# Feed-forward weight sums moved from POOL to DVE, and more eight-product blocks, in a two-layer diffusion step

## The chip, the core and the metric

The kernel runs on one core of one Trainium2 chip. The time is the device time of one execution in microseconds (us), and less is better. The core has a matrix engine (PE, with its weight loads shown as PEld), three engines for element-wise work (DVE, ACT and POOL), and queues that issue transfers; SP issues nearly all of them here. Each engine works through its own instructions in a fixed order, and waits at an instruction until the results that it needs are there.

## The reference, cut to what matters

One inference step of a two-layer backbone over 640 tokens: 512 latent tokens and 128 prompt tokens, which have a modulation of their own. Every layer is a mixer followed by a SwiGLU feed-forward part:

```python
def ada_modulation(cond, w_mod, b_mod):
    m = jax.nn.silu(cond) @ w_mod + b_mod          # 1024 -> 6 * 1024, one vector per group and layer
    return jnp.split(m, 6, axis=-1)                # sh1, sc1, g1, sh2, sc2, g2

def swiglu(h, w_in, w_out):
    gate, up = jnp.split(h @ w_in, 2, axis=-1)     # w_in 1024 x 5632, w_out 2816 x 1024
    return (jax.nn.silu(gate) * up) @ w_out

for l in range(2):
    ...
    hp = modulate(rms_norm(xp, norm_mix[l]), sh1_p, sc1_p)
    ...                                            # mixer: MLA + neighbourhood attention, or GQA
    hp = modulate(rms_norm(xp, norm_ffn[l]), sh2_p, sc2_p)
    xp = xp + g2_p * swiglu(hp, w_ffn_in[l], w_ffn_out[l])   # the same for the latent tokens xs
```

Everything is float32. The outputs are both streams after a final norm, and the context tensors of the two mixers.

## The kernel before, in words

**Arithmetic.** Tokens lie on the free axis (640 columns, two halves of 320), features on the 128 partitions, 1024 features in 8 tiles. A float32 product is made of three matmuls in a reduced 32-bit format: every operand is split into a high part (ACT copies it into that format) and a low part (DVE or POOL subtracts the high part from the source), and `mm3` adds high*high, high*low and low*high.

**Feed-forward, first half (`ffn`).** The 2816 hidden features are 22 blocks of 128. A block needs gate and up, each for two halves of the tokens and 8 tiles of features.

- The first `FEW` = 2 blocks of each layer take the plain way, eight products of four tiles: 2 (gate, up) x 2 (halves) x 8 (tiles) x 3 = 96 matmuls of 320 columns. Only the two raw weight tiles of 128 x 1024 are split (`unit`, L161 to L170).
- The other 20 blocks take seven products of four tiles (a Winograd scheme over gate and up, halves of the features and halves of the tokens): 7 x 4 x 3 = 84 matmuls. For that the weights are also added up: `s13` and `s24`, four additions of 128 x 512 on POOL (L1117, L1118, L1121, L1122), and `wX`, `wY`, `wZ`, `wW` are split (L1034, L1035, L1114, L1115). The activations are added up once a layer (`ModS.add_up`, L296 to L303, into the tiles D, C, N and E), between matmuls of block 0 in the order of the source.
- A block ends with a silu on ACT, the product `sg` (L1084 or L1098 on DVE), its split into `hd` (L1055 on ACT, L1056 on DVE), and, for most blocks, two transfers to DRAM (L1061, "spill"), since the chip's memory does not hold all of the hidden features.

`ModS.make` produces the activations of each half (`i` = 0, 1) that the products read: DVE multiplies by the norm (L280), ACT applies scale and shift (L283), and the split is on DVE (L289, L290) for even tiles and on POOL (L286, L287) for odd ones. The second half (`i` = 1) is made while PE is in block 0.

**Modulation as side work.** The modulation vectors of layer 1, and the last gate of layer 0, are not made by PE but by DVE, beside the feed-forward part: 48 weight tiles in layer 0 and 8 in layer 1. Each is loaded (`wm`, 512 KB), multiplied by the broadcast condition `cb`, and summed over its row by two instructions (`junk`, L1265). `mod_side` holds the list, and `step("fb", fb)` at the end of a block, or `step("n", i)` in the output layer, takes as many tiles as the plan says. `cb` lies where `ModS` keeps half of its sums, so that it can be loaded only after `add_up`.

**Rooms.** Raw weight tiles, `wm` among them, go through a ring of three rooms (tag `raw` of `rawp`); the second raw tile of a seven-product block has two rooms of its own (`wr`). Split weights have three rooms in `wp` and three in a pool that lives as long as the first half (`fp`); a plain block past the first takes both of its tiles from `wp`.

**Feed-forward, second half.** `wout` loads and splits the output weights in two passes over the 8 tiles of features (9 and 13 hidden blocks), alternating between `wp` and a pool `fo` that can open only when `fp` is free.

**Order.** The source gives dependencies and priorities. A planner then simulates the program with estimated durations, and writes out a fixed order for every engine and for every queue; where the thing first in the source is expected late, it puts other work ahead. Transfers of SP are issued in that fixed order too, each after the room that it fills is free.

Of the kernel before, what the change touches and what calls it, by code (L numbers as in the profile page):

```python
# [18 lines left out]
P = 128  # L19
# [29 lines left out]
def body(ctx, tc, xT, vecs, crow, wm0, wm0g, wm1, wA, wNV, wNA, wMK, wMV, wOA, wGQ, wGK, wGV, wOC,  # L49
# [3 lines left out]
    V, S, G = nc.vector, nc.scalar, nc.gpsimd  # L53
# [110 lines left out]
    def unit(src, n, name, lo="v", pool=None):  # L164

        raw = load(src, n, name + "r")
        t = (pool or wp).tile([P, 2, 1024], F32R, tag="w", bufs=3, name=name)
        hi, lw = t[:, 0, :n], t[:, 1, :n]
        S.activation(hi, raw, AF.Copy)
        (V if lo == "v" else G).tensor_tensor(lw, raw, f(hi), ALU.subtract)  # L170
        return hi, lw
# [77 lines left out]
    class ModS:  # L249
# [26 lines left out]
        def make(self, i, rs, k):  # L276
            h, l = self.hl(k, i)
            c0, c1 = HALF[i]
            t = tp.tile([P, HT], F32, tag="u", bufs=7, name=f"{self.name}t{k}{i}")
            V.tensor_tensor(t, self.x[k][:, c0:c1], rs[:, c0:c1], ALU.mult)  # L280
            h32 = (self.left, self.right)[i][k]
            for a0, a1, c in HCOND[i]:
                self.act[k, i] = S.activation(h32[:, a0 - c0:a1 - c0], t[:, a0 - c0:a1 - c0], AF.Identity,  # L283
                                              bias=self.ml[:, self.sh + k, c:c + 1], scale=self.gsl[:, k, c:c + 1])
            if k % 2:
                G.tensor_scalar(h, h32, 1.0, 0.0, ALU.mult, ALU.add)  # L286
                G.tensor_tensor(l, h32, f(h), ALU.subtract)  # L287
            else:
                V.tensor_copy(h, h32)  # L289
                V.tensor_tensor(l, h32, f(h), ALU.subtract)  # L290

        def add_up(self, k):
            left = [self.left[j] for j in (k, k + 4)]
            b12, b22 = self.right[k], self.right[k + 4]
            n = tp.tile([P, HT], F32, tag="u", bufs=7, name=f"{self.name}n{k}")
            V.tensor_tensor(b22, b22, b12, ALU.subtract)  # L296
            V.scalar_tensor_tensor(n, b22, -1.0, left[0], ALU.mult, ALU.subtract)
            V.tensor_tensor(left[0], left[0], b12, ALU.subtract)
            V.scalar_tensor_tensor(left[1], n, -1.0, left[1], ALU.mult, ALU.subtract)
            for c, src in zip("DNCE", (left[0], n, b22, left[1])):  # L300
                t = self.sums[c][k]
                S.activation(t[:, 0:HT], src, AF.Copy)
                (V if c in "DN" else G).tensor_tensor(t[:, HT:T], src, f(t[:, 0:HT]), ALU.subtract)  # L303

    def residual(xo, xi, ps, ml, g, n, i):

# [261 lines left out]
    for kk in range(4):  # L568
        wh, wl = unit(wNV[kk], 1024, f"wnv{kk}")
        for j in range(2):  # L570
            k = 2 * kk + j
# [432 lines left out]
                box["m"].make(c, nrm.rs, k)  # L1004
        return box, nxt

    FEW = 2
    STAY = 3
    FIRST, SECOND = FO_ORDER[:9], FO_ORDER[9:]

# [15 lines left out]
    def ffn(l, x, pend, hm, nxt, side, opened):  # L1026
        ph, fk, dr, hd, fs, fp, w0, _ = opened
        turn = [0]
# [9 lines left out]
        def whole(ps, wt, k, c, first, last):  # L1038
            a, b = [w[:, k * P:k * P + P] for w in wt]
            mm3(ps[:, :HT], a, b, *hm.hl(k, c), first, last)  # L1040
# [23 lines left out]
                kept[fb] = dh, dl  # L1064

        step = None
        for fb in range(FEW):
            pg, pu = [bank(f"fg{l}_{fb}{c}") for c in range(2)], pair(f"fu{l}_{fb}")
            g_, u_ = w1 if fb else w0
            for c in range(2):  # L1070
                for k in range(KT):
                    if fb == 0 and c == 0 and k == 3:
                        pend()
                        step = side(fk, hm.act[7, 1])
                        w1 = [after(hm.act[3 + 2 * i, 1], lambda: unit(wFI[l, 1, i], 1024, f"wgu{l}_1{i}")) for i in range(2)]
                        for j in range(4):
                            hm.add_up(j)
                    for ps, wt in ((pg, g_), (pu, u_)):
                        whole(ps[c], wt, k, c, k == 0, k == KT - 1)
            sg = tmp(f"sg{l}_{fb}")  # L1080
            for c, (c0, c1) in enumerate(HALF):
                after(hm.act[7, 1], lambda: S.activation(sg[:, c0:c1], pg[c][:, :HT], AF.Silu))
            for c, (c0, c1) in enumerate(HALF):
                V.tensor_tensor(sg[:, c0:c1], pu[c][:, :HT], sg[:, c0:c1], ALU.mult)  # L1084
            hidden(fb, sg)
            step("fb", fb)
# [13 lines left out]
            step("fb", fb)  # L1100

        job = None
        for fb in range(FEW, FB):

            ru = load(wFI[l, fb, 1], 1024, f"wu{l}_{fb}r")
            if fb == FEW:
                rg = load(wFI[l, fb, 0], 1024, f"wg{l}_{fb}r")
            else:
                rg = fp.tile([P, 1024], F32, tag="wr", bufs=2, name=f"wg{l}_{fb}r")
                nc.sync.dma_start(rg, wFI[l, fb, 0])  # L1110
            wX = split(ru, f"wX{l}_{fb}")
            t = fp.tile([P, 2, 512], F32R, tag="w4", bufs=2, name=f"wW{l}_{fb}")
            wW = t[:, 0, :], t[:, 1, :]
            S.activation(wW[0], rg[:, 512:], AF.Copy)  # L1114
            V.tensor_tensor(wW[1], rg[:, 512:], f(wW[0]), ALU.subtract)  # L1115
            s13 = fp.tile([P, 1024], F32, tag="ws", bufs=2, name=f"s13{l}_{fb}")
            G.tensor_tensor(s13[:, :512], rg[:, :512], rg[:, 512:], ALU.add)  # L1117
            G.tensor_tensor(s13[:, 512:], ru[:, :512], rg[:, :512], ALU.add)  # L1118
            wY = split(s13, f"wY{l}_{fb}")
            s24 = fp.tile([P, 1024], F32, tag="ws", bufs=2, name=f"s24{l}_{fb}")  # L1120
            G.tensor_tensor(s24[:, :512], s13[:, 512:], rg[:, 512:], ALU.add)  # L1121
            G.tensor_tensor(s24[:, 512:], s24[:, :512], ru[:, 512:], ALU.add)  # L1122
            wZ = split(s24, f"wZ{l}_{fb}")

            g, b5, b2 = bank(f"fg{l}_{fb}"), bank(f"fd{l}_{fb}"), bank(f"fu{l}_{fb}", "y")
            up, sg = tmp(f"up{l}_{fb}"), tmp(f"sg{l}_{fb}")
            p1, p5, u1, g2 = [utile(f"{n}{l}_{fb}") for n in ("p1", "p5", "u1", "g2")]
            product(g, wX, 0, 11, True)
            S.activation(p1, g[:, :HT], AF.Copy)  # L1129
            product(b5, wY, 0, "D", True)  # L1130
            S.activation(p5, b5[:, :HT], AF.Copy)
            if job:
                close(job)
            product(g, wZ, 0, "N", False)
            S.activation(u1, g[:, :HT], AF.Copy)  # L1135
            product(b2, wX, 512, 21, True)
            V.tensor_tensor(up[:, 0:HT], b2[:, :HT], p1, ALU.add)
            product(b5, wZ, 512, 22, False)
            V.tensor_tensor(up[:, HT:T], b5[:, :HT], u1, ALU.add)
            product(g, wY, 512, "C", False)  # L1140
            V.tensor_tensor(g2, g[:, :HT], p5, ALU.add)  # L1141
            S.activation(sg[:, HT:T], g2, AF.Silu, scale=-1.0)
            job = fb, g, wW, up, sg
# [19 lines left out]
        def wout(j0, n, tiles, name):  # L1163

            turn[0] += 1
            raw = (rawp.tile([P, 1024], F32, tag="raw", name=name + "r") if turn[0] % 2 else
                   fo.tile([P, 1024], F32, tag="raw", bufs=1, name=name + "r"))
            nt = len(tiles)
            nc.sync.dma_start(raw[:, :nt * n * P].rearrange("p (a b) -> p a b", a=nt),
                              wFO[l, tiles[0]:tiles[0] + nt, :, j0 * P:(j0 + n) * P].rearrange("a p b -> p a b"))  # L1170
            t = (wp.tile([P, 2, 1024], F32R, tag="w", bufs=3, name=name) if turn[0] % 2 else
                 fo.tile([P, 2, 1024], F32R, tag="w", bufs=2, name=name))
            m = nt * n * P
            S.activation(t[:, 0, :m], raw[:, :m], AF.Copy)
            V.tensor_tensor(t[:, 1, :m], raw[:, :m], f(t[:, 0, :m]), ALU.subtract)
            return [(t[:, 0, i * n * P:(i + 1) * n * P], t[:, 1, i * n * P:(i + 1) * n * P]) for i in range(nt)]
# [98 lines left out]
    def x_again(n):  # L1275
# [7 lines left out]
    x, pend = mixer_out(wOA, oMs + oNs, [4, 5, 6, 7, 0, 1, 2, 3], x_again, mods[0], "oa", nxt, op[-1])  # L1283
    box2, nxt = next_mod("h10", gs[1][0], mods[1], SH1)
    side = mod_side([(0, wm0g, G2)] + [(1, wm1[j:j + 8], j) for j in (SH1, SC1, G1, SH2, SC2)],
                    lambda kind, i: int(i > 4) + (i in (8, 11, 14, 17, 20)) if kind == "fb" else 1 + (i in (3, 5, 7)) if i < 8 else 2 + (i < 11) if i < 14 else 1)
    x, pend = ffn(0, x, pend, box["m"], nxt, side, op)


# [368 lines left out]
```

## Time and profile before

| | |
|---|---|
| Median of 3 runs | 1647.08 us (1644.03 to 1647.15) |
| Profiled execution | 1641.38 us, of which the span from first to last instruction is 1639.6 us |
| Mean granted clock of PE | 0.974 |
| Busy: PE, DVE, ACT, POOL | 92%, 70%, 45%, 34% of the span |
| Layer 0, feed-forward: first half, second half | from 417.4 to 759.3 us, to 914 us |
| Layer 1, feed-forward: first half, second half | from 1163.9 to 1473.6 us, to 1629 us |

In a row of windows, a stretch of the span is followed by its length, and by the busy time and the number of instructions of each engine. In a row of instructions, the numbers after the shape are the shortest, the median and the longest duration in ns, and the first and last start in us. In a timeline, a row gives start, duration, engine, line and tiles, and in brackets how long the engine was idle before it and what ended that.

### The profile page before, as it was taken

The numbers are of one execution on the slowest core, as the hardware profiler recorded it, in microseconds if no ns is written. First come the engines' busy times: TensorE is split into PE (matmuls) and PEld (weight loads), VectorE is DVE, ScalarE is ACT, GpSimd is POOL, SyncE is SP. The second block draws the span as 40 slices with busy tenths as digits, with TensorE's granted clock in tenths as the row PEclk, the third lists the DMA queues.
The fourth block names the chain that finished last, engine by engine and source line by source line (L and its number), as shares of the span: only waits on it lengthen the run. The fifth ranks groups of instructions, "written<-read, shape, count | busy, mean of one in ns | idle before, by whom it ended". The sixth has DMA issues, their size and how long they took to land.

```text
span 1639.6 us, 25446 instructions
## 1 busy us (share of the span) xinstructions
PE 1512.3 (92%) x9808; PEld 1434.6 (87%) x9808; DVE 1153.3 (70%) x1921; ACT 742.9 (45%) x1418; POOL 555.0 (34%) x498
## 2 busy tenths in 40 slices
PE   5999979999979888899999999999879999999997
PEld 3888858889868888889999989989868899999997
DVE  5656666875978898894895787784789867753333
ACT  4436566763544444342122556673544455541221
POOL 1225524522565455530000443222465555410000
PEclk9999979999979999999999999999999999999998
DMA  9334430004144544448863220002144443448311
GB/s 351 100 101 150 167 112 27 27 29 139 39 148 152 177 169 144 164 158 299 284 225 123 72 71 27 27 27 79 37 151 167 160 151 126 148 151 303 96 49 65
DMA packets 72970, 212.65 MB, mean 130 GB/s; under 512 B 8096, under 2 KB 12976, under 8 KB 72592
## 3 DMA queue, kind: packets, MB, share of 16 engines
q1 hardware_dynamic: 70080, 204.78, 36.7%
q10 hardware_dynamic: 2352, 5.31, 1.0%
q8 instruction: 77, 1.26, 0.3%
q0 software_dynamic: 416, 0.93, 0.2%
q14 instruction: 45, 0.37, 0.1%
HBM read 182.53 MB, written 28.46 MB: 129 GB/s over the span
## 4 chain that ended last, share of the span: by engine, by line
PE 56%; DVE 21%; DMA 10%; ACT 6%; issue 5%; POOL 2%; SPq 0%; ACTq 0%; DVEq 0%; POOLq 0%
PE fo L61 9%; PE fg L61 8%; DVE junk L1265 4%; DMA wm<-in_wm 4%; PE fd L61 3%; PE gq L61 2%; DMA wm<-in_wm0g 2%; DVE sg L1098 2%; PE nk L61 2%; PE nq L61 2%; PE fu L61 2%; DVE wX L1035 2%; PE mod L61 2%; PE go L61 1%; PE fo_2a L61 1%
## 5 line engine op out<-in xcount | busy, mean ns | idle before, releaser
L1265 DVE SCALAR_TENSOR_TENSOR junk<-wm,cb 128x1024 bf16<-128x1024 f32 x112 | 168.6, 1505 | 37.1 <-DMA wm<-in_wm 22.5
L1098 DVE TENSOR_TENSOR sg<-up,sg 128x640 f32<-128x640 f32 x40 | 62.1, 1553 | 49.0 <-ACT sg L1097 49.0
L61 PE MATMUL fg<-h01C,wY 128*128 128x320 f32 x240 | 43.7, 335 | 27.3 <-ACT u L1135 27.3
L61 PE MATMUL gq<-h10h,wgq 128*128 128x320 f32 x256 | 65.7, 315 | 0.2
L61 PEld LDWEIGHTS fg<-h01C,wY 128*128 128x128 f32 x240 | 38.5, 203 | 31.1 <-ACT u L1135 31.0
L244 POOL TENSOR_SCALAR h10h<-h10t,gs,mods 128x320 fp32r<-128x320 f32 x4 | 3.5, 876 | 182.8 <-DVE h10t L238 181.1
L1035 DVE TENSOR_TENSOR wY<-s,wY 128x1024 fp32r<-128x1024 f32 x40 | 60.3, 1507 | 1.8 <-ACT wY L1034 0.8
L1035 DVE TENSOR_TENSOR wZ<-s,wZ 128x1024 fp32r<-128x1024 f32 x40 | 50.5, 1263 | 7.6 <-ACT wZ L1034 7.6
L1034 ACT ACTIVATE wY<-s 128x1024 fp32r<-128x1024 f32 x40 | 42.4, 1059 | 22.5 <-PE fg L61 19.6
L1034 ACT ACTIVATE wZ<-s 128x1024 fp32r<-128x1024 f32 x40 | 42.1, 1053 | 20.0 <-PE fd L61 10.3
L61 PE MATMUL fg<-h11C,wY 128*128 128x320 f32 x240 | 41.2, 323 | 6.2 <-ACT u L1135 6.2
L61 PEld LDWEIGHTS gq<-h10h,wgq 128*128 128x128 f32 x256 | 44.7, 188 | 1.6 <-PE gtp L65 1.0
L61 PE MATMUL fg<-h01N,wZ 128*128 128x320 f32 x240 | 40.9, 322 | 5.4 <-ACT p L1129 5.4
L61 PE MATMUL fg<-h11N,wZ 128*128 128x320 f32 x240 | 40.1, 317 | 5.8 <-ACT p L1129 5.8
L61 PEld LDWEIGHTS fg<-h11C,wY 128*128 128x128 f32 x240 | 37.8, 197 | 7.4 <-ACT u L1135 7.4
L309 DVE SCALAR_TENSOR_TENSOR xr<-fo,mods,xr 128x320 f32<-128x320 f32 (+2 forms) x48 | 19.6, 436 | 35.0 <-PE fo L61 34.9
L61 PE MATMUL fd<-h01D,wY 128*128 128x320 f32 x240 | 40.0, 316 | 4.5 <-DVE wY L1035 4.5
L61 PE MATMUL fd<-h11D,wY 128*128 128x320 f32 x240 | 39.9, 316 | 4.5 <-DVE wY L1035 4.5
L61 PEld LDWEIGHTS fg<-h01N,wZ 128*128 128x128 f32 x240 | 37.9, 197 | 6.0 <-ACT p L1129 6.0
L61 PEld LDWEIGHTS fg<-h11N,wZ 128*128 128x128 f32 x240 | 37.4, 195 | 6.3 <-ACT p L1129 6.3
L61 PE MATMUL fg<-h01E,wW 128*128 128x320 f32 x240 | 39.0, 311 | 3.8 <-DVE g L1141 3.8
L61 PE MATMUL fg<-h01q,wX 128*128 128x320 f32 x240 | 41.9, 327 | 0.0
(3026 smaller groups left out, 5552.7 us busy)
## 6 DMA issues: line engine op xcount, KB each, us to landing
wm<-in_wm SPq DMA_DIRECT2D x48, 512.0 KB, 4.1
mraw<-in_wm SPq DMA_DIRECT2D x24, 512.0 KB, 3.9
mraw<-in_wm SPq DMA_DIRECT2D x8, 1024.0 KB, 15.3
wm<-in_wm0g SPq DMA_DIRECT2D x8, 512.0 KB, 4.5
x<-in_xT SPq DMA_DIRECT2D x8, 320.0 KB, 5.3
xr<-in_xT SPq DMA_DIRECT2D x8, 320.0 KB, 5.1
cb<-in_crow ACTq DMA_DIRECT2D x2, 1024.0 KB, 7.1
gt<-in_rpbp SPq DMA_DIRECT2D x8, 240.0 KB, 3.7
```

What stands on the lines that cost most here:

```text
L61: cls.last = nc.tensor.matmul(*a, **k)
L244: G.tensor_scalar(h[:, c0:c1], t, self.gsl[:, k, 0:1], self.ml[:, self.sh + k, 0:1], ALU.mult, ALU.add)
L309: V.scalar_tensor_tensor(xo[:, c0:c1], ps[:, c0 - o:c1 - o], ml[:, g + n, c:c + 1], xi[:, c0:c1], ALU.mult, ALU.add)
L1034: S.activation(t[:, 0, :], src, AF.Copy)
L1035: V.tensor_tensor(t[:, 1, :], src, f(t[:, 0, :]), ALU.subtract)
L1098: V.tensor_tensor(sg, up, sg, ALU.mult)
L1265: V.scalar_tensor_tensor(junk, raw, 1.0, cb[:, c, :], ALU.mult, ALU.mult, accum_out=mods[l][:, j0 + i, c:c + 1])
```

## The change

- The four additions of `s13` and `s24` are issued on DVE; so are the low parts of the sums C and E in `add_up`.
- For the second half of the tokens, `ModS.make` splits on ACT (high) and DVE (low) for all tiles; POOL and the DVE copy are no longer used there.
- `FEW` becomes 9 for layer 0 and 4 for layer 1. Plain blocks past the second load and split their own two tiles through `rawp` and `wp`.
- `add_up` comes after the matmuls of blocks 0 and 1 in the source, two tiles each.
- The side work of layer 0 is planned anew: none for blocks 0 to 2, then 3, 4, 3, 4, 3, 4 for blocks 3 to 8, one at every third of the later blocks, one for each of the first eight steps of the output layer, and two for each of the others. The plan of layer 1 is unchanged.
- `wout` takes the rooms of `wp` for both of its first two calls.

```diff
@@ ModS.make
-            if k % 2:
+            if i == 1:
+                S.activation(h, h32, AF.Copy)
+                V.tensor_tensor(l, h32, f(h), ALU.subtract)
+            elif k % 2:
@@ ModS.add_up
-                (V if c in "DN" else G).tensor_tensor(t[:, HT:T], src, f(t[:, 0:HT]), ALU.subtract)
+                V.tensor_tensor(t[:, HT:T], src, f(t[:, 0:HT]), ALU.subtract)
@@
-    FEW = 2
+    FEW = 9, 4
@@ ffn, plain blocks
-        for fb in range(FEW):
+        few = FEW[l]
+        for fb in range(few):
             pg, pu = [bank(f"fg{l}_{fb}{c}") for c in range(2)], pair(f"fu{l}_{fb}")
-            g_, u_ = w1 if fb else w0
+            if fb > 1:
+                g_, u_ = [unit(wFI[l, fb, i], 1024, f"wgu{l}_{fb}{i}") for i in range(2)]
+            else:
+                g_, u_ = w1 if fb else w0
             ...
-                        for j in range(4):
-                            hm.add_up(j)
                     for ps, wt in ((pg, g_), (pu, u_)):
                         whole(ps[c], wt, k, c, k == 0, k == KT - 1)
+            if fb in (0, 1):
+                for j in (2 * fb, 2 * fb + 1):
+                    hm.add_up(j)
@@ ffn, seven-product blocks
-        for fb in range(FEW, FB):
+        for fb in range(few, FB):
-            if fb == FEW:
+            if fb == few:
-            G.tensor_tensor(s13[:, :512], rg[:, :512], rg[:, 512:], ALU.add)
-            G.tensor_tensor(s13[:, 512:], ru[:, :512], rg[:, :512], ALU.add)
+            V.tensor_tensor(s13[:, :512], rg[:, :512], rg[:, 512:], ALU.add)
+            V.tensor_tensor(s13[:, 512:], ru[:, :512], rg[:, :512], ALU.add)
-            G.tensor_tensor(s24[:, :512], s13[:, 512:], rg[:, 512:], ALU.add)
-            G.tensor_tensor(s24[:, 512:], s24[:, :512], ru[:, 512:], ALU.add)
+            V.tensor_tensor(s24[:, :512], s13[:, 512:], rg[:, 512:], ALU.add)
+            V.tensor_tensor(s24[:, 512:], s24[:, :512], ru[:, 512:], ALU.add)
@@ wout
-            raw = (rawp.tile(...) if turn[0] % 2 else fo.tile(...))
+            early = len(tiles) > 1 or turn[0] % 2
+            raw = (rawp.tile(...) if early else fo.tile(...))
-            t = (wp.tile(...) if turn[0] % 2 else fo.tile(...))
+            t = (wp.tile(...) if early else fo.tile(...))
@@ the plan of the side work in layer 0
-  lambda kind, i: int(i > 4) + (i in (8, 11, 14, 17, 20)) if kind == "fb" else 1 + (i in (3, 5, 7)) if i < 8 else 2 + (i < 11) if i < 14 else 1
+  lambda kind, i: (0, 0, 0, 3, 4, 3, 4, 3, 4)[i] if kind == "fb" and i < 9 else int(i % 3 == 0) if kind == "fb" else 1 if i < 8 else 2
```

More of the change, by code (lines that the diff above doesn't have):

```diff
@@ L1165, in wout @@
             turn[0] += 1
-            raw = (rawp.tile([P, 1024], F32, tag="raw", name=name + "r") if turn[0] % 2 else
+            early = len(tiles) > 1 or turn[0] % 2
+            raw = (rawp.tile([P, 1024], F32, tag="raw", name=name + "r") if early else
                    fo.tile([P, 1024], F32, tag="raw", bufs=1, name=name + "r"))
@@ L1170, in wout @@
                               wFO[l, tiles[0]:tiles[0] + nt, :, j0 * P:(j0 + n) * P].rearrange("a p b -> p a b"))
-            t = (wp.tile([P, 2, 1024], F32R, tag="w", bufs=3, name=name) if turn[0] % 2 else
+            t = (wp.tile([P, 2, 1024], F32R, tag="w", bufs=3, name=name) if early else
                  fo.tile([P, 2, 1024], F32R, tag="w", bufs=2, name=name))
@@ L1285, in body @@
     side = mod_side([(0, wm0g, G2)] + [(1, wm1[j:j + 8], j) for j in (SH1, SC1, G1, SH2, SC2)],
-                    lambda kind, i: int(i > 4) + (i in (8, 11, 14, 17, 20)) if kind == "fb" else 1 + (i in (3, 5, 7)) if i < 8 else 2 + (i < 11) if i < 14 else 1)
+                    lambda kind, i: (0, 0, 0, 3, 4, 3, 4, 3, 4)[i] if kind == "fb" and i < 9 else int(i % 3 == 0) if kind == "fb" else 1 if i < 8 else 2)
     x, pend = ffn(0, x, pend, box["m"], nxt, side, op)
```

## The prediction

> **What bounds the kernel now.** I read the page's first section, then windows cut at the stages, then waits and timelines where PE loses time.
>
> ```profile
> PE 1512.3 (92%) x9808; PEld 1434.6 (87%) x9808; DVE 1153.3 (70%) x1921; ACT 742.9 (45%) x1418; POOL 555.0 (34%) x498
> ```
>
> PE is the bound on average. The windows (stretch, length, busy time of PE, PEld, DVE, ACT, POOL with counts, granted clock) tell where it is not:
>
> ```profile
> 417.40:451.50 34.10, 31.11 (x196) 28.68 (x195) 31.67 (x50) 20.95 (x44) 21.35 (x22) 1.00 0.15 47
> 451.50:759.30 307.80, 266.80 (x1693) 260.74 (x1692) 256.25 (x297) 128.76 (x209) 147.40 (x79) 0.94 0.49 166
> 759.30:914.00 154.70, 154.32 (x1049) 153.64 (x1048) 110.92 (x194) 36.57 (x54) 3.71 (x4) 1.00 0.62 211
> 1163.90:1198.20 34.30, 30.91 (x197) 28.78 (x196) 31.86 (x50) 22.01 (x45) 21.17 (x22) 1.00 0.15 46
> 1198.20:1298.40 100.20, 80.92 (x495) 78.14 (x493) 91.66 (x100) 42.90 (x68) 58.55 (x31) 0.93 0.49 167
> 1298.40:1470.70 172.30, 172.30 (x1178) 172.30 (x1177) 118.41 (x126) 88.23 (x137) 73.90 (x48) 1.00 0.40 139
> 1470.70:1629.00 158.30, 158.05 (x1072) 156.93 (x1070) 55.61 (x99) 32.64 (x48) 0.00 (x0) 1.00 0.41 137
> ```
>
> ```profile
> 1310.00:1460.00 150.00, 150.00 (x1025) 1.00 0.38 130
> ```
>
> The last row is a stretch without a gap: a matmul of 320 columns costs 150.00 / 1025 = 0.1463 us. A seven-product block (84) is then 12.29 us of PE and a plain one (96) 14.05 us. Length less count times 0.1463 is what PE loses in each window: 5.4, **60.1**, 1.2, 5.5, **27.8**, 0.0 and 1.5 us. So all that can be won lies in the seven-product blocks of layer 0 and in the first six or so of layer 1. The granted clock, 0.94 and 0.93 there and 1.00 where PE has no gaps, is part of these two numbers. How a loss arises, in a timeline of DVE, POOL, ACT and PE in layer 0:
>
> ```profile
> 588.50 1.70 DVE L1265 SCALAR_TENSOR_TENSOR junk<-wm,cb 128x1024 bf16<-128x1024 f32 x1 [1.80 <-DMA wm<-in_wm]
> ...
> 590.24 2.19 DVE L1265 SCALAR_TENSOR_TENSOR junk<-wm,cb 128x1024 bf16<-128x1024 f32 x1
> ...
> 592.36 1.87 DVE L1098 TENSOR_TENSOR sg<-up,sg 128x640 f32<-128x640 f32 x1
> ```
>
> ```profile
> 589.20 2.15 POOL L1121 TENSOR_TENSOR s<-s,wg_12r 128x512 f32<-128x512 f32 x1
> 591.42 2.13 POOL L1122 TENSOR_TENSOR s<-s,wu_12r 128x512 f32<-128x512 f32 x1
> ```
>
> ```profile
> 594.26 0.74 ACT L1055 ACTIVATE hd_0h<-sg 128x640 fp32r<-128x640 f32 x1 [6.72 <-DVE sg L1098]
> 594.91 0.42 ACT L1135 ACTIVATE u<-fg 128x320 f32<-128x320 f32 x1
> ```
>
> ```profile
> 595.38 0.64 PE L61 MATMUL fg<-h01C,wY 128*128 128x320 f32 x1 [3.55 <-ACT u L1135]
> ```
>
> DVE waits 1.80 us for a modulation tile, then runs three instructions that POOL's additions stretch; ACT stands 6.72 us at `hd`, which needs `sg`; behind it in ACT's order is `u`, and PE waits 3.55 us for that. The prices of the same work, free and held (shortest, median, longest ns):
>
> ```profile
> L1265 DVE SCALAR_TENSOR_TENSOR junk<-wm,cb x112: 1207/1225/2319, 484.2 to 1290.5; 128x1024 bf16<-128x1024 f32 x112
> L1098 DVE TENSOR_TENSOR sg<-up,sg x40: 811/1887/1933, 488.6 to 1474.1; 128x640 f32<-128x640 f32 x40
> L1056 DVE TENSOR_TENSOR hd_2l<-sg,hd_2h x14: 812/826/827, 492.1 to 1466.0; 128x640 fp32r<-128x640 f32 x14
> L1137 DVE TENSOR_TENSOR up<-fu,p x40: 476/484/492, 473.4 to 1467.5; 128x320 f32<-128x320 f32 x40
> L1035 DVE TENSOR_TENSOR wX<-wu_12r,wX x2: 1226/1226/1226, 596.3 to 1333.1; 128x1024 fp32r<-128x1024 f32 x2
> L1115 DVE TENSOR_TENSOR wW<-wg_13r,wW x2: 678/678/679, 622.4 to 1355.4; 128x512 fp32r<-128x512 f32 x2
> L1115 DVE TENSOR_TENSOR wW<-wg_10r,wW x2: 677/1230/1783, 578.0 to 1317.6; 128x512 fp32r<-128x512 f32 x2
> L1122 POOL TENSOR_TENSOR s<-s,wu_13r x2: 1284/1522/1761, 607.0 to 1341.2; 128x512 f32<-128x512 f32 x2
> L1084 DVE TENSOR_TENSOR sg<-fu_0a,sg x2: 478/479/480, 452.9 to 1199.6; 128x320 f32<-128x320 f32 x2
> ```
>
> DVE's 512 columns take 0.68 us free and 1.78 held, the 640 of `sg` 0.81 and 1.9. Without POOL, DVE needs for a seven-product block 3 x 1.22 + 0.68 + 2 x 0.82 + 3 x 0.48 = 7.4 us. The four additions on POOL, 1.28 each at the least, make 12.5 if the two engines take turns, which is just what 12.29 us of PE bears (no loss after 1298); a modulation tile (2 x 1.225 = 2.45) brings it to 15.
>
> **The change part by part.**
>
> *Additions on DVE.* No row has this addition on DVE; the nearest is `wW`, the same shape with two inputs: 0.68 us (ends: 0.48, the row of 320 columns, and 1.78, the held one). I take 0.68, since nothing on POOL is left to hold it. DVE: 7.4 + 4 x 0.68 = 10.1 us of 12.29; with a tile 12.6 by durations.
>
> The Trainium skill speaks against the move on its page Perfetto Trace Analysis (Optimizing Scalar/DVE Operations): a saturated DVE may be relieved by giving work to other engines, though it adds that between DVE and GpSimd this might not help. By the first half, the sum would be +2.7 us of DVE a block and nothing back; by its page SBUF — State Buffer (Who interferes with whom), where one of the two blocks wholly while the other reads through the shared port, it is 12.5 us of taking turns against 10.1. The held rows above agree with the second.
>
> *More plain blocks.* 7 + 2 blocks x 12 matmuls x 0.1463 = **+15.8 us** of PE, on the path.
>
> *Tiles beside plain blocks.* A plain block needs of DVE 2 x 1.22 + 2 x 0.48 + 0.82 = 4.2 us, and 3.5 tiles on average for blocks 3 to 8. Each tile is 2.45 us and a wait for its transfer:
>
> ```profile
>   DMA wm<-in_wm: 22.5, 18
>   DMA wm<-in_wm0g: 12.0, 7
> ```
>
> ```profile
> L1265 DVE SCALAR_TENSOR_TENSOR junk<-wm,cb 128x1024 bf16<-128x1024 f32 x50 | 85.4, 1707 | 32.0 <-DMA wm<-in_wm 19.3 <-DMA wm<-in_wm0g 12.0
> ```
>
> Over all 56 tiles the wait is 34.5 / 56 = 0.62 us, in the stage itself 32.0 / 25 = 1.28. DVE then takes 15.0 to 17.3 us of a block, 0.9 to 3.2 above PE; I take 1.9, the middle, x 6 = **11.4 us** left of the loss in layer 0. Behind the waiting tile on DVE stand `sg` and the low part of the next weights; ACT waits for `sg`, and PE for both.
>
> *Rooms.* The ring of three serves tiles and weights, and SP stands at it in its order:
>
> ```profile
> SPq L161 <- DVE junk L1265: 78.0, 22, 4.5
> ```
>
> ```profile
> wm<-in_wm SPq DMA_DIRECT2D x48, 512.0 KB, 4.1
> ...
> cb<-in_crow ACTq DMA_DIRECT2D x2, 1024.0 KB, 7.1
> ...
> wu_12r<-in_wFI SPq DMA_DIRECT2D x2, 512.0 KB, 4.2
> ```
>
> ```profile
> L1034 ACT ACTIVATE wY<-s x40: 1040/1061/1064, 451.5 to 1446.4; 128x1024 fp32r<-128x1024 f32 x40
> ```
>
> A tile holds a room 4.1 + 2.45 = 6.6 us, a weight 4.2 + 1.06 + 1.22 = 6.5. Blocks 3 to 8 pass 21 tiles and 12 weights, 217 us of rooms: 72 us with three rooms turning, inside the 84.3 of PE; 109 with two. A plain block past the first takes both its split tiles from the three rooms of `wp`, so the up weights get the room that the gate weights of the block before leave at its end: copy 1.06 and subtraction 1.22 after that. The like is in the trace for block 1:
>
> ```profile
> 437.53 0.89 PE L61 MATMUL fg<-h01q,wgu 128*128 128x320 f32 x5
> 438.81 0.85 PE L61 MATMUL fu_1a<-h01q,wgu 128*128 128x320 f32 x4 [0.39 <-DVE wgu L170]
> ```
>
> The planner pulled gate matmuls ahead (x5, not x3) and PE lost 0.4 us. Ends: 0 (24 gate matmuls are 3.5 us of cover) and 2.3 (none used); I take 0.7, near the row, x 7 = 4.9 in layer 0 and 1.4 in layer 1, and once more at each first seven-product block. Transfers keep their number; 33 of 512 KB and 12 spills of 320 KB in 84 us are 250 GB/s, above the 211 that the output layer bears without loss, one more reason not to take the low end of the tiles' wait.
>
> *Later blocks.* In layer 0 every third has one tile, 12.6 of 12.29 us with two lighter ones beside: 0. In layer 1 blocks 4 to 9 have one each, with waits 13.2 to 13.9 by durations, while starts follow each other up to 0.1 us earlier than ends (590.24 + 2.19 against 592.36): between 0 and 1.6, I take 0.5 x 6 = 3.0.
>
> *Activations and their sums.*
>
> ```profile
> L302 ACT ACTIVATE h01N<-h01n x4: 454/456/456, 435.8 to 454.2; 128x320 fp32r<-128x320 f32 x4
> L287 POOL TENSOR_TENSOR h01q<-h0132d,h01q x3: 866/989/1052, 422.9 to 429.3; 128x320 fp32r<-128x320 f32 x3
> L303 POOL TENSOR_TENSOR h01C<-h0132u,h01C x4: 923/956/1015, 436.7 to 455.1; 128x320 fp32r<-128x320 f32 x4
> ```
>
> For the second half, eight copies of 0.46 go to ACT (+3.7 us of its 20.95 in 34.10) and eight subtractions of 0.48 to DVE; POOL's 0.99 for every odd tile goes. Ends -3 (POOL's turns gone) and +3.7 (ACT is the chain); I take 0 and keep 5.4 and 5.5 us of loss. The low parts of C and E are 8 x 0.48 = 3.8 us more on DVE, hidden in blocks 1 and 2, which use 4.2 of 14.05; uncovered, 3.8. `cb` may load once the sums are done, 7.1 us and a silu, within block 2.
>
> *Output layer.* It has four tiles fewer, and lost 1.2 us: gain 0 to 1.2, I take 0. Two tiles now come at its step 14, where DVE has slack:
>
> ```profile
> 902.24 0.55 DVE L309 SCALAR_TENSOR_TENSOR xr<-fo,mods,xr 128x320 f32<-128x320 f32 x1 [4.13 <-PE fo L61]
> ```
>
> Uncovered they cost 4.9 - 4.1 = 0.8. The rooms of `wout`: 0.
>
> **Sum.** Layer 0 keeps 11.4 + 4.9 + 0.7 = 17.0 of 60.1: -43.1. Layer 1 keeps 1.4 + 3.0 + 0.7 = 5.1 of 27.8: -22.7. PE +15.8. Together **-50.0 us**: the profiled execution of 1641.4 becomes 1591. It stands 5.7 under the median of 1647.1, from which the forecast is **1597 us**.
>
> **The rivals.**
>
> - *All of it is hidden*: both losses go but for nothing, 60.1 + 27.8 - 15.8 = 72.1, **1575 us**. For it: no loss after 1298 even with POOL at work. Against: 1.28 us of waits a tile.
> - *The ring is the bound* of blocks 3 to 8: a weight waits in its room for its place in `wp`, two rooms turn, 109 - 84.3 = 25 us instead of 11.4: **1611 us**. SP's 78 us at `junk` speak for it.
> - *Slower: the up weights wait.* If the planner puts three tiles ahead of the up weights' subtraction on DVE: 3 x 3.7 + 2.3 - 3.5 of cover = 10 us at each of six blocks, 60 for the 4 counted: **1653 us**. It decides from 9 us a block. Against it is the order at 437, where PE was given other work.
> - *Slower: DVE becomes the bound*, the change not doing what it says: at the held price of 1.78, a block is 14.5 us of DVE, 2.2 above PE, x 31 = 69: **1666 us**. It decides from 1.6 us an addition; POOL would have to be busy for it.
>
> **How the numbers follow.** The forecast has 0.60, all hidden 0.15, the ring 0.17, the two slower ones 0.05 and 0.03. The range from **1573 to 1622** takes in the first three, with 11 us beyond the ring for the ends of activations and boundaries; the slower two and some tails are left out. About 0.2% (3 us) is what a measurement of this kernel can tell: faster 0.92 from the first three cases, slower 0.07 and same 0.01 from the other two, since the up weights can also come out at no change.
>
> **What would show it.** Right: `sg` at 0.81 and `wW` at 0.68 throughout, the additions at 0.68 on DVE, plain blocks at 14 to 17 us, seven-product blocks at 12.3, clock 1.00 from block 9 on. Wrong: DVE idle for `wm` over 1.3 us a tile in blocks 3 to 8, PE waiting on `wgu`'s low part over 2 us a block, or additions over 1 us.

## Result and the profile after

The changed kernel takes 1581.16 us (median of 4 runs, 1580.52 to 1583.54) against 1646.36 us for the kernel before on the same chip: a ratio of 0.9609 with a 95% interval of 0.9592 to 0.9626. It is 65 us faster, where 50 were forecast. The profiled execution took 1580.5 us with a span of 1578.7, which is 60.9 less than the span before.

The first row of the profile after, and its windows at the same stages as before (the first two blocks of layer 0, its other plain blocks, its seven-product blocks, its output layer, then the same four of layer 1):

```profile
PE 1508.4 (96%) x9916; PEld 1435.7 (91%) x9916; DVE 1092.3 (69%) x2025; ACT 728.3 (46%) x1389; POOL 238.9 (15%) x306
```

```profile
418.70:452.00 33.30, 31.68 (x196) 28.71 (x195) 29.18 (x68) 26.05 (x57) 2.92 (x4) 1.00 0.19 64
452.00:558.60 106.60, 102.19 (x674) 100.00 (x673) 80.55 (x125) 27.77 (x39) 0.00 (x0) 0.98 0.70 230
558.60:722.90 164.30, 163.16 (x1111) 162.55 (x1110) 143.82 (x209) 84.29 (x132) 0.00 (x0) 1.00 0.53 174
722.90:875.90 153.00, 153.00 (x1044) 152.84 (x1044) 98.55 (x175) 36.64 (x54) 3.74 (x4) 1.00 0.58 197
1125.60:1158.90 33.30, 31.70 (x196) 28.73 (x195) 29.17 (x68) 26.06 (x57) 2.92 (x4) 1.00 0.17 64
1158.90:1190.40 31.50, 28.71 (x194) 28.18 (x193) 24.08 (x34) 13.27 (x17) 0.00 (x0) 1.00 0.69 230
1190.40:1410.20 219.80, 219.80 (x1502) 219.80 (x1501) 175.99 (x246) 112.92 (x176) 0.00 (x0) 1.00 0.46 150
1410.20:1567.90 157.70, 157.47 (x1072) 156.93 (x1070) 55.67 (x99) 32.53 (x48) 0.00 (x0) 1.00 0.41 137
```

PE has 108 matmuls more (9916 less 9808), 15.8 us. Length less count times 0.1463 leaves as loss 4.6, 8.0, 1.8, 0.3, 4.6, 3.1, 0.1 and 0.9 us: 23.4 in all, against 101.5 before. So the two stages that lost 60.1 and 27.8 us now lose 8.0 + 1.8 and 3.1 + 0.1. The sum of the windows, -78.1 + 15.8 = -62.3, is within 1.5 us of the change of the span.

The prices (count; shortest, median, longest ns) are free ones throughout. POOL, busy for 326 us in these stages before, has 9.6 us left there, none of it beside a block past the second:

```profile
L1106 DVE TENSOR_TENSOR sg<-up,sg x31: 818/824/827, 576.4 to 1413.6; 128x640 f32<-128x640 f32 x31
L1123 DVE TENSOR_TENSOR wW<-wg_9r,wW x2: 681/683/685, 557.9 to 1245.5; 128x512 fp32r<-128x512 f32 x2
L1125 DVE TENSOR_TENSOR s<-wg_9r x2: 684/687/690, 557.3 to 1228.4; 128x512 f32<-128x512 f32 x2
L1274 DVE SCALAR_TENSOR_TENSOR junk<-wm,cb x112: 1211/1224/1228, 464.0 to 1243.0; 128x1024 bf16<-128x1024 f32 x112
```

From first matmul to first matmul, the plain blocks of layer 0 take 18.95, 14.28, 14.65, **18.88**, 14.29, 14.36, 14.88, 15.27 and 14.35 us, and its seven-product blocks 13.18, then 12.31 up to the last (14.54, with matmuls of the output layer run inside it). Block 3 is the one large loss. Timelines of DVE and of PE (start, duration), and PE's granted clock just after the wait:

```profile
467.20 1.23 DVE L1274 SCALAR_TENSOR_TENSOR junk<-wm,cb 128x1024 bf16<-128x1024 f32 x1 [0.69 <-DMA wm<-in_wm0g]
...
470.08 1.23 DVE L1274 SCALAR_TENSOR_TENSOR junk<-wm,cb 128x1024 bf16<-128x1024 f32 x1 [0.39 <-DMA wm<-in_wm0g]
...
471.24 0.49 DVE L1092 TENSOR_TENSOR sg<-fu_2b,sg 128x320 f32<-128x320 f32 x1
471.64 1.22 DVE L170 TENSOR_TENSOR wgu<-wgu_31r,wgu 128x1024 fp32r<-128x1024 f32 x1
```

```profile
472.91 4.15 PE L61 MATMUL fu_3a<-h01q,wgu 128*128 128x320 f32 x16 [2.88 <-DVE wgu L170]
```

```profile
472.90:477.00 4.10, 4.09 (x17) 0.58 0.86 262
```

The low part of block 3's up weights (`wgu_31r`) comes at 471.64, behind modulation tiles and `sg` in DVE's order, and PE stands 2.88 us. The 16 matmuls after the wait take 4.15 us instead of 2.34, at a clock of 0.58. Wait and slow clock make 4.7 of the 4.8 us that block 3 takes over 14.05.

### The profile page after: what moved, and what is told of

Same layout as the page of the kernel before. It is cut to its first block, busy times and chain, and to the rows that moved or that the text cites. A ratio compares the mean times of both kernels' runs of the same rounds, so it can differ in the third digit from the quotient of the medians.

```text
span 1578.7 us, 25456 instructions
## 1 busy us (share of the span) xinstructions
PE 1508.4 (96%) x9916; PEld 1435.7 (91%) x9916; DVE 1092.3 (69%) x2025; ACT 728.3 (46%) x1389; POOL 238.9 (15%) x306
## 3 DMA queue, kind: packets, MB, share of 16 engines
q8 instruction: 78, 1.28, 0.3%
## 4 chain that ended last, share of the span: by engine, by line
PE 73%; DVE 13%; DMA 5%; ACT 5%; issue 3%; POOL 0%; DVEq 0%; ACTq 0%; SPq 0%; POOLq 0%
PE fg L61 14%; PE fo L61 10%; PE fd L61 7%; PE fu L61 3%; PE gq L61 2%; DMA wm<-in_wm 2%; DVE junk L1274 2%; PE nk L61 2%; PE nq L61 2%; PE mod L61 1%; PE go L61 1%; PE fo_2b L61 1%; PE fo_4b L61 1%; PE fo_2a L61 1%; PE fo_6b L61 1%
## 5 line engine op out<-in xcount | busy, mean ns | idle before, releaser
L61 PE MATMUL fg<-h01q,wgu 128*128 128x320 f32 x432 | 85.0, 313 | 0.9 <-DVE h01q L287 0.4
L61 PEld LDWEIGHTS fg<-h01q,wgu 128*128 128x128 f32 x432 | 68.1, 188 | 3.6 <-DVE h01q L287 2.1
L1106 DVE TENSOR_TENSOR sg<-up,sg 128x640 f32<-128x640 f32 x31 | 25.5, 823 | 25.4 <-ACT sg L1105 25.4
L61 PE MATMUL fg<-h11q,wgu 128*128 128x320 f32 x192 | 40.2, 318 | 0.9 <-DVE h11q L287 0.4
L1444 ACT ACTIVATE gp<-gs,gb,rq 128x640 f32<-128x640 f32 (+1 forms) x40 | 31.9, 796 | 19.2 <-DVE gb L1443 17.1
L61 PE MATMUL gq<-h10l,wgq 128*128 128x320 f32 x128 | 39.7, 310 | 0.0
L61 PE MATMUL fg<-h11E,wW 128*128 128x320 f32 x216 | 34.7, 310 | 0.0
L61 PE MATMUL fd<-h11q,wZ 128*128 128x320 f32 x216 | 34.6, 309 | 0.0
L61 PE MATMUL fg<-h11q,wX 128*128 128x320 f32 x216 | 34.6, 309 | 0.0
L61 PE MATMUL fu<-h11q,wX 128*128 128x320 f32 x216 | 34.6, 309 | 0.0
```

The costliest lines, as they stand in the source:

```text
L61: cls.last = nc.tensor.matmul(*a, **k)
L1106: V.tensor_tensor(sg, up, sg, ALU.mult)
L1444: S.activation(dst, src, AF.Exp, bias=nb, scale=rq[:, j:j + 1], accum_out=ll[:, j:j + 1])
```

## Experiments

The theory after the first result: the gain comes from taking the additions off POOL, because an instruction of POOL and a two-input instruction of DVE hold each other; the plain blocks and the new plan keep the tiles out of seven-product blocks and are paid for by 15.8 us of PE. The first rival: the plain blocks carry the gain, and without them DVE becomes the bound. Times are medians; the kernel before took 1646.5, 1648.3 and 1646.8 us beside the three groups of runs (e1 to e4, e5 to e8, e9 and e10).

**e1: the additions alone**, in the kernel before.

```diff
-            G.tensor_tensor(s13[:, :512], rg[:, :512], rg[:, 512:], ALU.add)
+            V.tensor_tensor(s13[:, :512], rg[:, :512], rg[:, 512:], ALU.add)
 # and the same for the other three of s13 and s24
```

> The kernel before, with the four additions of s13 and s24 on DVE and nothing else changed (two plain blocks a layer, the old plan of the tiles, the old activations). Theory, that POOL's work held DVE: a seven-product block needs 10.1 us of DVE, 12.6 with a tile, against 12.3 of PE and 15 before; the loss of 60.1 us in layer 0 falls to 20 to 35 (a third of the blocks have two tiles, and tiles wait 1.3 us), that of 27.8 in layer 1 to about 10: 1595 to 1615 us. Rival, that DVE was overfull by its own work and POOL merely shared it: DVE gets 2.7 us more a block, 1647 us or more. Under the first, sg takes 0.81 us and not 1.9.

Measured: 1568.66 us (1565.67 to 1568.98), ratio 0.9526 [0.9511, 0.954]. One part alone gives 77.8 us, more than the whole change, and the time is 26 us under the range expected: the losses fell further than the theory had it. The price of `sg` in e1, and the windows of its 20 seven-product blocks in layer 0 and in layer 1:

```profile
L1098 DVE TENSOR_TENSOR sg<-up,sg x40: 814/822/827, 475.9 to 1401.2; 128x640 f32<-128x640 f32 x40
```

```profile
453.30:707.50 254.20, 249.05 (x1694) 247.99 (x1693) 242.01 (x363) 131.47 (x202) 0.78 (x1) 1.00 0.59 196
1146.20:1400.70 254.50, 249.64 (x1688) 248.74 (x1688) 210.10 (x295) 130.29 (x202) 0.72 (x1) 0.99 0.48 162
```

The loss is 254.20 - 1694 x 0.1463 = 6.4 us and 7.5 us. It lies in the first seven-product block (17.60 and 19.50 us) and the last; all between take 12.31, those with two tiles too. DVE is busy for 95% of the first window, and in the blocks between PE does not wait for it.

The trace of the kernel before also tells whether POOL's sums were merely late. What PE waited for most in the seven-product blocks of layer 0 was not the weights made of them, but `u` (engine, what waited, for whom; total, times, longest in us):

```profile
PE fg L61 <- ACT u L1135: 27.3, 13, 3.6
```

`u` stands on ACT behind `hd`, and in that stretch ACT waited 82.0 us for `sg` of DVE and 6.3 us, once, for a sum of POOL. In the same stage of e1 it waits 2.6 us for `sg`.

**e2: the additions back on POOL**, in the changed kernel (the same four lines, `V` to `G`).

> The changed kernel, with the four additions of s13 and s24 back on POOL. Theory, that POOL held DVE: blocks without a tile take turns for 12.5 us, just at PE's 12.3, so lose 0 to 0.5 us each; the eleven seven-product blocks with a tile need 15 and lose 1.5 to 2.5 each: 1595 to 1612 us. Rival, that the plan (tiles beside plain blocks) brought the gain: within 5 us of 1581.

Measured: 1608.46 us (1599.98 to 1608.85), ratio 0.9759 [0.9732, 0.9786]. The price of `sg` in e2, and one wait of layer 1:

```profile
L1106 DVE TENSOR_TENSOR sg<-up,sg x31: 812/1871/1934, 588.9 to 1441.7; 128x640 f32<-128x640 f32 x31
```

```profile
PEld fg L61 <- ACT u L1143: 3.8, 1, 3.8
```

The held price is back, and so is the wait for `u`. The total is where it was expected, the way to it is not: of the 27.3 us between e2 and the changed kernel, some 26 lie in four blocks, not in all that hold a tile. These are the first two seven-product blocks of layer 0 (22.1 and 16.0 us, against 13.2 and 12.3) and the first and the third of layer 1, where PE stands up to 5.4 us for `p` or `u`. The rest of the change without the additions is worth 38.0 us, the additions alone 77.8, both together 65.2: the rest, taken as a whole, gains only as long as POOL is in the way.

**e3: other work on POOL.** The changed kernel with ten more additions of 128 x 128 per seven-product block on POOL, whose output nothing reads.

```diff
+            for j_ in range(10):
+                src_ = f(wW[0])[:, P * (j_ % 4):P * (j_ % 4) + P]
+                G.tensor_tensor(fp.tile([P, P], F32, tag="dup", ...), src_, src_, ALU.add)
```

> The changed kernel, plus ten additions of 128 x 128 on POOL in every seven-product block, of a weight tile that is in the chip's memory anyway, into a room of their own that nobody reads. They move no work and delay no result that anyone needs. Theory, that an addition on POOL holds a DVE instruction with two inputs: about 4.7 us of POOL a block come on top of DVE's 10.1, 14.8 against 12.3 of PE: 30 to 80 us more, 1611 to 1660 us, with sg well over 0.81 us. Rival, that POOL's sums were late rather than in the way: 1581 us, within 4.

Measured: 1593.83 us (1587.89 to 1598.37), ratio 0.968 [0.9653, 0.9708]; 12.7 us more than without, less than half of the low end expected. The added instructions, and `sg`:

```profile
L1134 POOL TENSOR_TENSOR dup<-wW x310: 399/730/1482, 559.5 to 1415.4; 128x128 f32<-128x128 f32 x155
```

```profile
L1106 DVE TENSOR_TENSOR sg<-up,sg x31: 812/826/1024, 580.6 to 1431.6; 128x640 f32<-128x640 f32 x31
```

Both sides are held although no data passes between them, but `sg` goes from 0.82 only to 1.02, where the 512-column additions took it to 1.9. So, as far as these two sizes show, what DVE loses per instruction goes with the length of the POOL instruction that it meets. That is the size which the expectation had wrong; its 4.7 us of POOL a block are 7.3 at the median of 0.73. Blocks of 12.9 to 14.1 us come in two rows of four, from 587 us in layer 0 and from 1216 us in layer 1; the others stay at 12.31, three of layer 0 that hold a tile among them. Why it is these blocks stays open.

**e4: fewer plain blocks**, one tile beside each block from block 3 in layer 0.

```diff
-    FEW = 9, 4
+    FEW = 3, 2
-  lambda kind, i: (0, 0, 0, 3, 4, 3, 4, 3, 4)[i] if kind == "fb" and i < 9 else int(i % 3 == 0) if kind == "fb" else 1 if i < 8 else 2
+  lambda kind, i: int(i > 2) if kind == "fb" else 1 + (i < 13)
```

> The changed kernel with three plain blocks in layer 0 and two in layer 1, and one tile beside every block of layer 0 from block 3 on, 29 beside its output layer. Theory, that a seven-product block without POOL bears one tile (12.6 us of DVE by durations, less by starts): eight plain blocks fewer are 8 x 1.76 = 14 us, 1567 us. Rival, that tiles cost the path 0.5 to 1 us each beside seven-product blocks because of their transfers, so that the plain blocks are needed: 10 to 19 us come back, 1577 to 1586 us.

Measured: 1569.80 us (1567.96 to 1570.16), ratio 0.9533 [0.9517, 0.9549], 11.4 better than the changed kernel. The first seven-product block of layer 0 has one wait of PE; it ends at 473.68 us:

```profile
PEld fg L61 <- ACT p L1137: 2.7, 1, 2.7
```

`p` waits on ACT behind `hd` of the block before, and that for `sg`, which comes at 471.98 on DVE, behind an instruction of a tile and additions for later blocks. This is the chain of the kernel before (`sg`, `hd`, then what PE needs) in a new place. Of the 18 blocks behind it 12 take 12.31 us, most with a tile; five in a row around 650 us grew by 0.35 to 2.2.

**e5: two plain blocks and the old plan**, with the rest of the change.

```diff
-    FEW = 9, 4
+    FEW = 2, 2
 # and the plan of the side work as in the kernel before
```

> The changed kernel with two plain blocks in both layers and the old plan of the tiles: additions on DVE, the new activations and their sums, the new rooms of wout. Theory, that the plain blocks and their plan are pure cost once POOL is out of the way: 9 x 12 matmuls x 0.1463 = 15.8 us less, and the 4 to 5 us that PE waits for up weights in blocks 3 to 7 of layer 0 and 2.8 in layer 1 go too, while the first seven-product block comes back with 2 to 5 us in each layer: 1560 to 1566 us. Rival, that the plain blocks give DVE time which the tiles need: the seven-product blocks of layer 0 lose 0.5 us or more each and eat the gain, 1570 us or more.

Measured: **1559.74 us** (1557.03 to 1561.71), ratio 0.9465 [0.9437, 0.9492], the best version with e10. Plain blocks 18.95 and 14.26, the first seven-product block 14.41 (14.58 in layer 1), all others 12.31 but the last. Windows of the seven-product blocks:

```profile
449.70:700.60 250.90, 248.93 (x1693) 247.84 (x1692) 238.62 (x356) 130.85 (x203) 0.00 (x0) 1.00 0.59 195
1140.70:1390.30 249.60, 248.16 (x1688) 247.23 (x1687) 209.10 (x295) 130.40 (x203) 0.00 (x0) 1.00 0.49 164
```

They lose 3.2 and 2.6 us with all of the old plan's tiles beside seven-product blocks. Why DVE can bear that stands in its timeline:

```profile
563.74 1.22 DVE L1274 SCALAR_TENSOR_TENSOR junk<-wm,cb 128x1024 bf16<-128x1024 f32 x1
564.88 0.08 DVE L1274 DVE_READ_ACCUMULATOR junk<-wm,cb 128x1 f32 x1
564.88 0.69 DVE L1125 TENSOR_TENSOR s<-wg_13r 128x512 f32<-128x512 f32 x1
565.49 0.68 DVE L1126 TENSOR_TENSOR s<-wu_13r,wg_13r 128x512 f32<-128x512 f32 x1
```

From 563.74 to 564.88 are 1.14 us, not 1.22; from 564.88 to 565.49 0.61, not 0.69. An instruction begins while the one before it is still recorded as running, so durations overstate what DVE needs: added up, this window's instructions make 264 us, 13 more than the window is long.

**e6: the up weights of plain blocks in rooms of `fp`**, which takes away the wait for a room of `wp`.

```diff
-  g_, u_ = [unit(wFI[l, fb, i], 1024, f"wgu{l}_{fb}{i}") for i in range(2)]
+  g_, u_ = [unit(wFI[l, fb, i], 1024, f"wgu{l}_{fb}{i}", pool=(wp, fp)[i]) for i in range(2)]
```

> The changed kernel, with the up weights of plain blocks past the second in the rooms of the pool fp, of which two are free after block 0, and the gate weights in wp as before. Theory, that PE waits in block 3 of both layers since the up weights get their room only at the end of the block before, and their subtraction stands behind tiles on DVE: the waits for wgu (3.2 at block 3, 0.7 and 1.1 at blocks 6 and 7 of layer 0, 2.8 in layer 1, with the half clock that follows the first) shrink to under 1 us in all, 1572 to 1576 us. Rival, that DVE or the ring of raw rooms is simply behind there: the same waits, 1581 us within 3.

Measured: 1584.98 us (1582.36 to 1587.75), ratio 0.9617 [0.9583, 0.9651]. All plain blocks from the third on take 13.97 to 14.14 us: the wait at block 3 is gone. But the first seven-product block takes 23.91 us (13.18 with the change), in layer 1 18.69. The waits of PE's weight loads in that block of layer 0, with ACT's and DVE's part in the longest:

```profile
PEld fg L61 <- ACT p L1137: 7.4, 1, 7.4
PEld fd L61 <- ACT wY L1037: 1.5, 1, 1.5
PEld fd L61 <- DVE wY L1038: 1.0, 1, 1.0
```

```profile
563.37 0.74 ACT L1058 ACTIVATE hd_0h<-sg 128x640 fp32r<-128x640 f32 x1 [2.15 <-DVE sg L1092]
564.02 0.42 ACT L1137 ACTIVATE p<-fg 128x320 f32<-128x320 f32 x1
```

```profile
561.71 1.22 DVE L1274 SCALAR_TENSOR_TENSOR junk<-wm,cb 128x1024 bf16<-128x1024 f32 x1
...
562.85 0.48 DVE L1092 TENSOR_TENSOR sg<-fu_8b,sg 128x320 f32<-128x320 f32 x1
```

The chain is that of e4: `sg` of block 8 stands on DVE behind a tile and the next blocks' additions, `hd` waits for it on ACT, `p` stands behind `hd`, and PE waits 7.4 us for `p`. The theory was right about block 3 and wrong about the time: the loss moved to the next boundary. Why the planner put `sg` that late in this order was not tried.

**e7: the old plan with the nine and four plain blocks** (only the line of the plan is undone).

> The changed kernel with nine and four plain blocks and the old plan of the tiles in layer 0 (none to block 4, then one a block, two at every third). Theory, that tiles need no plain blocks once the additions are on DVE: no wait for up weights at block 3 in layer 0, none in the seven-product blocks, so 4 to 7 us less, 1574 to 1577 us. Rival, that the new plan is what keeps the seven-product blocks free: two tiles at blocks 11, 14, 17 and 20 cost 1 to 3 us each, 1585 to 1593 us.

Measured: 1575.57 us (1571.39 to 1579.99), ratio 0.9562 [0.953, 0.9594]. Waits of PE's weight loads in the plain blocks of layer 0 after the first, then one in layer 1, whose plan is the same in both kernels:

```profile
PEld fg L61 <- DVE wgu L170: 0.6, 1, 0.6
PEld fu_8a L61 <- DVE wgu L170: 0.3, 1, 0.3
```

```profile
PEld fu_3a L61 <- ACT wgu L169: 3.3, 1, 3.3
```

Without tiles at block 3 of layer 0 it takes 14.29 us: the wait there needs the tiles (and, by e6, the rooms of `wp`). In layer 1 block 3 waits for ACT's copy of the up weights with either plan of layer 0. Between the medians of e7 and e5 lie 15.8 us, as much as the 108 matmuls; since e7's four runs spread over 8.6 us, that it fits to the tenth is luck. So the plan costs the change about 5.6 us, of which block 3 makes 4.6, and the plain blocks cost it their PE time and buy nothing.

**e8: activations and their sums as before** (the edits to `ModS.make` and `add_up` undone).

```diff
-            if i == 1:
-                S.activation(h, h32, AF.Copy)
-                V.tensor_tensor(l, h32, f(h), ALU.subtract)
-            elif k % 2:
+            if k % 2:
 # the low parts of C and E on POOL, add_up inside block 0
```

> The changed kernel with the activations as before: the split of odd tiles of the second half on POOL, the low parts of C and E on POOL, all of add_up in block 0. Theory, that this is worth little on its own: the first two blocks of each layer lose about 1 us more (5.4 and 5.5 before, 4.6 after), 1582 to 1585 us. Rival, that POOL holding DVE in the first two blocks delays the weights of what follows too: 5 us or more, 1586 us and up.

Measured: 1589.03 us (1585.88 to 1591.66), ratio 0.9643 [0.9614, 0.9671], 7.9 slower than the changed kernel, in the range of the rival. Windows of the first two blocks and the other plain blocks of layer 0, and its longest wait there:

```profile
417.40:451.60 34.20, 30.79 (x196) 28.61 (x195) 31.76 (x59) 23.38 (x49) 19.90 (x20) 1.00 0.17 59
451.60:564.10 112.50, 103.70 (x674) 101.02 (x673) 83.43 (x128) 28.64 (x39) 1.29 (x1) 0.97 0.65 221
```

```profile
PEld fu_3a L61 <- DVE wgu L170: 5.5, 1, 5.5
```

The first two blocks take 0.9 us more, as the theory had it; the larger part, 5.9 us, comes later, where the waits for `wgu` add up to 10.7 us, against 5.7 with the change (5.5 against 3.1 of it at block 3). Which of the three edits undone here makes them longer was not tried.

**e9: two tiles beside each of the later blocks**, on e5.

```diff
-  int(i > 4) + (i in (8, 11, 14, 17, 20)) if kind == "fb" else ...
+  2 * (i > 4) if kind == "fb" else 1
```

> The version with two plain blocks a layer, but with two modulation tiles beside every seven-product block of layer 0 from the sixth on (34 in 17 blocks, where it had 22), and one a step in the output layer. Theory (a DVE instruction costs its distance from start to start, 1.14 us for a junk of 1.22, so a block is 8.75 us of DVE and a tile 2.29): two tiles make 13.3 us of DVE against 12.3 of PE, so these blocks grow to about 13.3 and the time to 1559.7 + 17 x 1.0 = 1577 us (1572 to 1582). Rival A (the durations in the profile add up): 10.1 + 4.9 = 15.0 us, blocks grow by 2.7, 1559.7 + 46 = 1606 us. Rival B (DVE is not the bound, what a tile costs is only the wait for its transfer): blocks stay at 12.3, 1557 to 1562 us.

Measured: 1577.14 us (1576.28 to 1581.21), ratio 0.9584 [0.9556, 0.9613]. The total is the theory's, the way to it only in part. The same stretch of e5, then of e9, and e9's waits:

```profile
520.00:690.00 170.00, 170.00 (x1161) 170.00 (x1161) 161.93 (x246) 86.70 (x135) 0.00 (x0) 1.00 0.58 192
```

```profile
520.00:690.00 170.00, 164.51 (x1092) 159.82 (x1091) 167.36 (x262) 79.06 (x128) 0.00 (x0) 1.00 0.60 199
```

```profile
PEld fg L61 <- DVE wZ L1038: 5.3, 8, 0.7
PEld fd L61 <- ACT p L1139: 4.6, 7, 0.7
```

Now DVE is the bound, and PE waits for `wZ` or `p` in block after block. But only eight blocks ahead of the last grew, to 13.84 us as the median (12.31 + 1.5; expected +1.0 by starts, +2.7 by durations). The expectation's 8.75 us a block is itself too low: the distances from start to start in e5 (1.14 for 1024 columns, 0.74 for 640, 0.60 for 512, 0.40 for 320) add up to 9.1, and with two tiles to 13.7, near the 13.84. The eight blocks from 492 us on did not grow. They hold 3.4 `junk` instructions on the average instead of four, which is 13.0 us by starts, and the two before them hold one each, 10.2; DVE idles for less than 0.3 us in every one of them, so it had worked ahead. PE's loss in the blocks that grew is 11.5 of the 17.4 us. At the start of the output layer PE waits another 4.5 us for the first weights (e5 has 2.1 in that layer).

**e10: the rooms of the output weights as before**, on e5.

```diff
-            early = len(tiles) > 1 or turn[0] % 2
+            early = turn[0] % 2
```

> The version with two plain blocks a layer, but with the rooms of the output weights as before the change. Together with the version that has the additions alone (1568.7) it splits what is left between the two: activations and their sums, or the rooms. Theory (the rooms are worth nothing, as predicted; the activations give the 8 to 9 us): 1558 to 1563 us. Rival (the rooms of the output weights give them): 1566 to 1570 us, with a wait ahead of the first matmuls of the output layer.

Measured: 1559.41 us (1556.78 to 1560.73), ratio 0.947 [0.9447, 0.9492], the same as e5. The rooms are worth nothing, and what separates e1 from e5, about 9 us, is the activations and their sums. Most of it, 8.1 us, is in the seven-product blocks, at the first of each layer (17.60 and 19.50 us in e1, 14.41 and 14.58 in e5).

So one way through the runs, from the kernel before to the changed one, is: additions -77.8 (e1), activations -9 (e1 to e10), 108 matmuls +15.8 (e5 to e7), plan +5.6 (e7 to the change). That these add up to the -65.2 of the change proves nothing, since each step begins where the one before it ends; and in another order a part has another worth: put on last, the additions give 27.3 (e2).

## Why the prediction was right, and where it was off

The direction and the range held, and so did the main step of the mechanism, that DVE is free once POOL's additions are gone. But 1581.2 lies nearer to the rival in which all is hidden (1575) than to the forecast of 1597: two terms that were to eat up part of the gain did not come as worked out.

- *Additions at 0.68 us on DVE, nothing held*: right (0.69, `sg` 0.82). The two pages of the Trainium skill that were weighed come out as the held rows said. What the Trainium skill says in SBUF — State Buffer (Who interferes with whom) agrees with e2 (`sg` at 1.87) and e3 (1.02 at the most). The hint of the Trainium skill, Perfetto Trace Analysis (Optimizing Scalar/DVE Operations), to give work of a saturated DVE to other engines does not hold for this pair: e1 goes the other way and gains 77.8 us, which is the page's own reservation about DVE and GpSimd.
- *PE +15.8*: right (108 matmuls more in the trace, and 15.8 us from e5 to e7).
- *Tiles beside plain blocks 11.4, rooms 4.9, together 16.3*: **mis-sized**, 8.0 measured in that window. The step that failed is the 1.9 us a block that DVE was to need above PE's time (the middle of its 0.9 and 3.2 is 2.1, too). DVE's idle time ahead of tiles, from 452 to 559 us, is 11.9 us, or 0.6 for each of the 21 tiles, not up to 1.28:

```profile
L1274 DVE SCALAR_TENSOR_TENSOR junk<-wm,cb 128x1024 bf16<-128x1024 f32 x42 | 51.4, 1223 | 11.9 <-DMA wm<-in_wm 8.6 <-DMA wm<-in_wm0g 2.6
```

With that and its 73.3 us of busy time in blocks 3 to 8, DVE needs 14.2 us a block, and PE 14.05: hardly anything is left over to be lost. What was lost came by the mechanism of the term *Rooms*, a late low part of the next up weights: PE's waits for it are 4.4 us in all (2.9 of them at block 3) and the slow clock behind the longest 1.8. It is the rival "the up weights wait", at one block in layer 0 instead of six, and with it came, at this block alone, the prediction's sign of being wrong (over 2 us). In layer 1 block 3 waited too, behind ACT:

```profile
PEld fu_3a L61 <- ACT wgu L169: 2.7, 1, 2.7
```

- *Layer 1: 5.1 left*: 3.2 measured. The term of 3.0 for one tile beside blocks 4 to 9 was 0.1. It came from adding up durations; from start to start a `junk` costs 1.14 and an addition 0.61, which puts a block with one tile, at 11.4 us, below PE's 12.29. The prediction saw the 0.1 us between starts and ends, and took 0.5 us a block where carrying it through the sum leaves 0. The Trainium skill, Perfetto Trace Analysis (Optimizing Scalar/DVE Operations), says that the recorded DVE latency is about twice an overhead of some 60 ns, since the second half overlaps with the next instruction; the 0.08 us of e5's timeline are near it.
- *Activations: 0 of -3 to +3.7*: mis-sized. In the first two blocks of each layer it was -1.7 (4.6 of 5.4 and 5.5 left), and -8 to -9 with what follows (e8, e10).
- *Output layers: 0*: -1.5 measured (1.2 to 0.3, and 1.5 to 0.9). The rooms of `wout` at 0 are confirmed by e10.
- *Clock 1.00 from block 9 on*: right (1.00 in every later window).

The terms miss by 8.3 + 1.9 + 1.7 + 1.5 us, less 1.1 for the seven-product blocks of layer 0 (1.8 lost, at the first and the last, against 0.7): 12.3. Outside the windows 1.4 went the other way, and the profiled execution, 1580.5 against 1591.4, is the 10.9 between them. The rest of the distance of the medians is the 5.7 us by which the profiled execution before stood under its median, which the forecast added and which the one after does not show (0.6).

What the prediction never asked is whether the plain blocks are needed once POOL is out of the way. By durations a seven-product block with a tile is 12.6 us of DVE against 12.29, by which they look useful; on the chip e5 does without them and is 21 us faster than the change.

## What to carry to other kernels

Where DVE and POOL each look affordable by themselves, look for two prices of one instruction (0.82 and 1.9 us here): then the work that POOL takes over costs DVE more than it saves. When a change has a cure for the cause and a bypass around the symptom, price the bypass again without the cause; here it cost 21 us. And take what an engine needs per block from start to start of its instructions, not from their durations: at some 15 instructions a block the difference decided whether DVE or PE was the bound.

## What was not expected of the hardware

- How much DVE loses to POOL goes with POOL's instruction: +0.20 us per instruction beside additions of 128 x 128 (e3), about +1.1 beside those of 128 x 512 (e2). And not every instruction with two inputs loses: `up`, which reads one of its two from the memory where PE leaves its results, never takes more than 0.49 us, neither in e2 and e3 nor in the kernel before.
- A wait of 2.88 us in layer 0 was followed by matmuls at a granted clock of 0.58 for 4 us; one of 2.47 us at block 3 of layer 1 was not, as the window behind it shows (PE alone, clock, DMA):

```profile
1177.40:1181.20 3.80, 3.80 (x26) 1.00 0.65 187
```

  The Trainium skill, TensorE: Matmul & The Clock Gate (What's actually happening), puts the threshold at an idle window of about 3.4 us that runs freely; here a shorter wait was enough. Nor does the length alone decide: a wait of 2.12 us in e1 (until 1156.72) was followed by a clock of 0.52, one of 2.46 us in e4 (until 473.68) by 1.00.
- The busy share does not tell how near DVE is to its bound. In the same 170 us in which e9's DVE is busy for 167.4 us and blocks grow by 1.5, DVE in e1 is busy for 167.9 (with 253 instructions, not 262), and no block grows:

```profile
520.00:690.00 170.00, 167.90 (x253) 1.00 0.57 189
```
